# Seven products instead of eight for each 2x2 block in the second weights of the feed-forward and gated parts

## The chip, the cores and the metric

One Trainium2 chip, one NeuronCore of it. The metric is the device time of one execution of the whole program in microseconds (us); of several runs the median counts. One execution was also recorded by the hardware profiler, and all durations below come from that one.

## What is computed

Two small transformers, one after the other, on one sequence of 512 tokens with 1024 features, all in float32. The change touches four of their parts: twice `sqrelu_mlp` (4096 hidden features) and twice `swiglu` (2816 hidden features). Everything else (convolutions, three kinds of attention, norms) stays as it is.

```python
def sqrelu_mlp(h, w1, w2):
    return jnp.square(jax.nn.relu(h @ w1)) @ w2

def swiglu(h, w_gate, w_up, w_down):
    return (jax.nn.silu(h @ w_gate) * (h @ w_up)) @ w_down

# in both models, for each of two layers:
    h = rmsnorm(x, norm_ff_g[l]);  x = x + sqrelu_mlp(h, ff_w1[l], ff_w2[l])
    h = rms_norm(x, ffn_norm[i]);  x = x + swiglu(h, ffn_w_gate[i], ffn_w_up[i], ffn_w_down[i])
```

## The kernel before, in words

The activations lie transposed in SBUF: the residual `x` is eight tiles of 128 features by 512 tokens. A matmul takes 128x128 weights as its stationary operand and streams a 128x512 activation tile. Full float32 precision comes from splitting: each operand is a rounded high part (ScalarE, `nc.scalar.copy`) and the rest as a low part (VectorE, a subtraction), and `mm3` (line 171) issues three matmuls for each product: high x high, high x low, low x high. Each of the three loads its own weights.

`load_weights` (line 144) brings two columns of weight tiles (eight tiles deep, 1 MB) into one of three `raw` buffers. `split_weights` (line 161) makes `whi` on ScalarE (line 167) and `wlo` on VectorE (line 168). There are two tags, a and b, that alternate with every second call, with two buffers each; a new `whi` has to wait until TensorE has read the old contents of its buffer. `gemm_steps` (line 180) takes two output tiles at a time, goes over the hidden tiles k, and evacuates each PSUM bank at the end.

The feed-forward part (`ff_sqrelu`, line 672) goes over four chunks of eight hidden tiles. For each chunk it multiplies by the first weights (`ff_w1`), makes the hidden tiles (line 684 on VectorE, 686 on ScalarE, split at 215 and 216), and multiplies them by the second weights (`ff_w2`), adding the outcome to `x` (line 574 on VectorE). The gated part (`swiglu`, line 696) does the same with chunks of 8, 8 and 6 hidden tiles, where two first weights make each hidden tile. So the second weights of one chunk of eight are 8 x 8 products of 128x128 by 128x512, which are 192 matmuls.

A scheduler at build time puts the instructions of VectorE, ScalarE, GpSimd and the DMA queue into an order; TensorE's order is the program's. On the chip each engine takes its instructions in that order, and one that waits holds up those behind it.

Of the kernel before, what the change touches and what calls it, by code (L numbers as in the profile page):

```python
# [9 lines left out]
F32 = mybir.dt.float32  # L10
F32R = mybir.dt.float32r
# [69 lines left out]
def model_kernel(tc, a, c_mats, c_onehot, c_lnn, out):  # L81
# [497 lines left out]

    def memory_attention(l, st):  # L580
# [91 lines left out]
    def ff_sqrelu(l, st, last=None):  # L672
        nrm = Norm(st)
        with ExitStack() as s:
            ap = pool("fact", 22, s)
            fp = pool("fftmp", stack=s)
            h = [gained_act(hp_all, x[k], gain("norm_ff_g", l)[:, k : k + 1]) for k in range(KT)]
            st2 = Stats()
            for hc in range(FF1 // D):
                hid = []  # L680

                def evac(m, acc, hid=hid):
                    t = fp.tile([P, T], F32, name="t", tag="t", bufs=4)
                    nc.vector.scalar_tensor_tensor(t, acc, 0.0, nrm.b, op0=OP.max, op1=OP.mult)  # L684
                    u = fp.tile([P, T], F32, name="u", tag="u", bufs=4)
                    nc.scalar.activation(u, t, AF.Square)
                    hid.append(split_act(ap, u))

                gemm(cols(a["ff_w1"][l], 0, hc * D), h, evac, first=hc == 0, hooks=nrm.hooks() if hc == 0 else ())
                final = hc == FF1 // D - 1  # L690
                gemm(
                    cols(a["ff_w2"][l], hc * D, 0), hid, (last or residual(st2)) if final else residual(None), first=True
                )
        return st2

    def swiglu(l, st, last=None, finish=None):
        nrm = Norm(st)
        banks(4, 2, 2)
        with ExitStack() as s:
            ap = pool("gact", 22, s)  # L700
# [3 lines left out]
            wg, wu, wd = a["ffn_w_gate_2"][l], a["ffn_w_up_2"][l], a["ffn_w_down_2"][l]  # L704
            m0 = 0
            for n in (8, 8, 6):
                hid = []
                for j in range(n):
                    c = (m0 + j) * P
                    res = {}  # L710

                    def evac(m, acc, res=res, hid=hid):
                        if m == 0:
                            t = fp.tile([P, T], F32, name="t", tag="t", bufs=4)
                            nc.vector.tensor_tensor(t, acc, nrm.b, op=OP.mult)  # L715
                            g = fp.tile([P, T], F32, name="g", tag="g", bufs=4)
                            nc.scalar.activation(g, t, AF.Silu)  # L717
                            nc.gpsimd.tensor_tensor(g, g, nrm.b, op=OP.mult)  # L718
                            res[0] = g
                        else:  # L720
                            u = fp.tile([P, T], F32, name="u", tag="u", bufs=4)
                            nc.vector.tensor_tensor(u, acc, res[0], op=OP.mult)  # L722
                            hid.append(split_act(ap, u))
# [3 lines left out]
                final = m0 + n == FF2 // P  # L727
                n_cols = 6 if final and finish else KT
                gemm(cols(wd, m0 * P, 0, n_cols), hid, (last or residual(st2)) if final else residual(None), first=True)
                if n_cols < KT:  # L730
                    finish(cols(wd, m0 * P, n_cols * P, KT - n_cols), hid)
# [548 lines left out]
    with ExitStack() as s:  # L1280
        cp = pool("sconv", stack=s)
# [59 lines left out]
    def finish(specs, acts):  # L1341
# [23 lines left out]
        def tokens(half):  # L1365
            for t in range(2 * half, 2 * half + 2):
                for j in range(2):
                    b = bank("gs"[j])
# [51 lines left out]
```

## Time and profile before

| what | value |
|---|---|
| median of 3 runs | 2662.1 us (2660.45 to 2663.39) |
| the profiled execution's own time | 2659.51 us |
| its span, first to last instruction | 2657.7 us |
| TensorE busy | 2605.3 us, 98% of the span, 12521 matmuls |
| VectorE busy | 1489.1 us, 56% |
| ScalarE busy | 1096.9 us, 41% |
| GpSimd busy | 555.0 us, 21% |
| mean granted TensorE clock | 0.994 |

TensorE is busy nearly all the time, so time comes or goes only where its stream of matmuls gets shorter, gets slower, or has to wait. "Busy" of a matmul counts from its start to its modelled end, and neighbours overlap; the work that TensorE does is read from the distance between the starts of neighbours, not from the durations. A row of the timeline has start, duration, engine, line, operation, output and inputs, shape, count and, in brackets, the idle time before and what ended it.

### The profile page before, as it was taken

To read this page: it belongs to the slowest core of one execution; us is meant where nothing else is said; L and a number is where in the kernel's file an instruction comes from. 1 tells how busy PE (TensorE), PEld (TensorE's weight loads), DVE (VectorE), ACT (ScalarE), POOL (GpSimd) and SP (SyncE) were. 2 spreads that over 40 slices of the span, in tenths; PEclk is the share of its full clock that TensorE was granted. 3 is DMA by queue.
4 is the path that set the end of the run, shared out by engine and by line. 5 is a ranking of instruction groups with operands and counts; after the bars stand their busy time and mean duration, and the time that the engine had idled before them with its cause. 6 is when DMAs were issued, how large, how long until landed. Compare 5 with 4: busy or idle time off the path is not lost.

```text
span 2657.7 us, 32286 instructions
## 1 busy us (share of the span) xinstructions
PE 2605.3 (98%) x12521; PEld 2184.0 (82%) x12521; DVE 1489.1 (56%) x2215; ACT 1096.9 (41%) x1843; POOL 555.0 (21%) x586
## 2 busy tenths in 40 slices
PE   8999999999999999999999999999999999999999
PEld 6889888888878877888888788878888888788888
DVE  6995664443558887554344665343335777643333
ACT  6755443322337665442223323232224666422223
POOL 5862120000226532110000501111112221210111
PEclk9999999999999999999999999999999999999999
DMA  7255133233322322233333233843323323233331
GB/s 211 83 197 181 48 111 95 95 95 95 96 77 68 100 76 72 78 105 103 102 97 95 80 95 97 114 142 102 100 86 111 92 84 90 76 96 99 95 87 56
DMA packets 318057, 264.82 MB, mean 100 GB/s; under 512 B 6741, under 2 KB 304273, under 8 KB 317905
## 3 DMA queue, kind: packets, MB, share of 16 engines
q1 hardware_dynamic: 313808, 252.90, 31.3%
q0 software_dynamic: 1616, 5.52, 1.9%
q10 hardware_dynamic: 2480, 4.33, 0.5%
q8 instruction: 99, 1.62, 0.2%
q14 instruction: 54, 0.43, 0.0%
HBM read 251.16 MB, written 11.57 MB: 99 GB/s over the span
## 4 chain that ended last, share of the span: by engine, by line
PE 56%; DVE 2%; DMA 2%; issue 1%; ACT 1%; POOL 0%; ACTq 0%; DVEq 0%; POOLq 0%
PE ps_g L90 52%; DMA raw<-in_ffn_w_gate 2%; PE ps_s L90 2%; PE ps_t L90 1%; PE ps_t L93 1%; DVE wlo L168 0%; DVE x L1261 0%; DVE alo L228 0%; POOL ssq L252 0%; DVE x L574 0%; ACT ahi L227 0%; DVE x L1259 0%; DVE x L916 0%; ACT sq L248 0%; DVE wlo L773 0%
## 5 line engine op out<-in xcount | busy, mean ns | idle before, releaser
L90 PE MATMUL ps_g<-ahi,whi 128*128 128x512 f32 x3052 | 1196.5, 392 | 9.2 <-DVE x L574 4.9
L90 PE MATMUL ps_g<-ahi,wlo 128*128 128x512 f32 x3052 | 1190.2, 390 | 0.0
L90 PE MATMUL ps_g<-alo,whi 128*128 128x512 f32 x3052 | 1189.7, 390 | 0.0
L167 ACT CAST whi<-raw 128x1024 fp32r<-128x1024 f32 (+2 forms) x384 | 384.1, 1007 | 1115.2 <-PE ps_g L90 1035.3
L90 PEld LDWEIGHTS ps_g<-ahi,whi 128*128 128x128 f32 x3052 | 575.8, 189 | 127.8 <-issue 5.6
L90 PEld LDWEIGHTS ps_g<-ahi,wlo 128*128 128x128 f32 x3052 | 575.2, 188 | 121.7 <-DVE wlo L168 0.8
L90 PEld LDWEIGHTS ps_g<-alo,whi 128*128 128x128 f32 x3052 | 575.8, 189 | 115.4
L168 DVE TENSOR_TENSOR wlo<-raw,whi 128x1024 fp32r<-128x1024 f32 (+2 forms) x384 | 463.8, 1213 | 78.1 <-ACT whi L167 73.4
L574 DVE TENSOR_TENSOR x<-ps_g,x 128x512 f32<-128x512 f32 x144 | 99.2, 689 | 337.5 <-PE ps_g L90 337.4
L252 POOL TENSOR_TENSOR ssq<-ssq,sq 128x512 f32<-128x512 f32 x78 | 121.3, 1556 | 609.0 <-issue 313.7
L718 POOL TENSOR_TENSOR g<-g,rb 128x512 f32<-128x512 f32 x44 | 74.4, 1691 | 566.3 <-ACT g L717 566.3
L684 DVE SCALAR_TENSOR_TENSOR t<-ps_g,rb 128x512 f32<-128x512 f32 x64 | 44.1, 691 | 171.9 <-PE ps_g L90 171.9
L760 POOL TENSOR_TENSOR raw<-raw,gcols 128x512 f32<-128x512 f32 x48 | 53.9, 1147 | 304.3 <-DMA raw<-in_kvf_w 304.3
L414 POOL TENSOR_TENSOR pa<-pa,pr 128x512 f32<-128x512 f32 x80 | 111.8, 1400 | 18.7 <-ACT pa L410 8.2
L722 DVE TENSOR_TENSOR u<-ps_g,g 128x512 f32<-128x512 f32 x44 | 30.4, 691 | 141.9 <-PE ps_g L90 135.7
L406 DVE SCALAR_TENSOR_TENSOR ps_s<-u,gcols,ps_s 128x512 f32<-128x512 f32 x152 | 104.2, 744 | 0.2
L972 POOL TENSOR_SCALAR sall<-sall,rs 128x512 f32<-128x512 f32 (+3 forms) x128 | 75.9, 604 | 129.9 <-DVE rs L971 118.8
L773 DVE TENSOR_TENSOR wlo<-raw,whi 128x512 fp32r<-128x512 f32 x128 | 95.2, 772 | 13.5 <-ACT whi L770 13.4
L770 ACT CAST whi<-raw 128x512 fp32r<-128x512 f32 x128 | 74.1, 620 | 53.5 <-PE ps_g L90 47.4
L715 DVE TENSOR_TENSOR t<-ps_g,rb 128x512 f32<-128x512 f32 x44 | 30.4, 690 | 114.5 <-PE ps_g L90 114.5
L228 DVE SCALAR_TENSOR_TENSOR alo<-x,gcols,ahi 128x512 fp32r<-128x512 f32 x64 | 81.0, 1277 | 13.7 <-ACT ahi L227 13.7
L216 DVE TENSOR_TENSOR alo<-u,ahi 128x512 fp32r<-128x512 f32 x116 | 79.5, 689 | 1.4 <-ACT ahi L215 1.4
(245 smaller groups left out, 2843.7 us busy)
## 6 DMA issues: line engine op xcount, KB each, us to landing
raw<-in_ff_w SPq DMA_DIRECT2D x64, 1024.0 KB, 4.9
raw<-in_ffn_w_gate SPq DMA_DIRECT2D x44, 512.0 KB, 3.9
raw<-in_ffn_w_up SPq DMA_DIRECT2D x44, 512.0 KB, 5.2
raw<-in_ffn_w_down SPq DMA_DIRECT2D x16, 1024.0 KB, 5.1
raw<-in_conv_pw_w SPq DMA_DIRECT2D x16, 512.0 KB, 5.4
raw<-in_mem_wk SPq DMA_DIRECT2D x8, 1024.0 KB, 4.9
raw<-in_mem_wv SPq DMA_DIRECT2D x8, 1024.0 KB, 5.4
raw<-in_mem_wq SPq DMA_DIRECT2D x8, 1024.0 KB, 4.8
```

What stands on the lines that cost most here:

```text
L90: tc.keep_in_program_order(nc.tensor.matmul(*args, **kw))
L167: nc.scalar.copy(hi, view)
L168: nc.vector.tensor_tensor(lo, view, hi.bitcast(F32), op=OP.subtract)
L216: nc.vector.tensor_tensor(lo, src, hi.bitcast(F32), op=OP.subtract)
L228: nc.vector.scalar_tensor_tensor(lo, src, g, hi.bitcast(F32), op0=OP.mult, op1=OP.subtract)
L252: nc.gpsimd.tensor_tensor(self.ssq, self.ssq, dst, op=OP.add)
L406: nc.vector.scalar_tensor_tensor(acc, u[:, j : j + T], tapw(j), acc, op0=OP.mult, op1=OP.add)
L414: nc.gpsimd.tensor_tensor(pa, pa, pr, op=OP.add)
L574: nc.vector.tensor_tensor(x[m], acc, x[m], op=OP.add)
L718: nc.gpsimd.tensor_tensor(g, g, nrm.b, op=OP.mult)
L773: nc.vector.tensor_tensor(w[1][:, k0 : k0 + n, :], v, w[0][:, k0 : k0 + n, :].bitcast(F32), op=OP.subtract)
L972: pinned(nc.gpsimd.tensor_scalar(s, s, rs[:, i : i + 1], 1.0, op0=OP.mult, op1=OP.mult))
```

## The change

In every chunk but the last of each of the four parts (three of four in the feed-forward part, two of three in the gated part: ten chunks in all), the product with the second weights is made by a scheme of seven products (Strassen's, in Winograd's form) over blocks of two hidden tiles by two output tiles by two halves of the tokens (256 each). The weights of such a block are a11, a21, a12, a22 (row: even or odd hidden tile, column: first or second output tile).

- `Hidden` (line 596) holds one pair of hidden tiles: `quarters` (line 616) keeps three of the four quarters and makes four differences and sums of them on VectorE, then splits all seven into `hi` and `lo`. In the last chunk `tile` (line 611) splits the whole tile as before.
- `Seven` (line 631) holds four accumulators in SBUF. `weights` (line 638) makes, for a pair of output tiles and four pairs of hidden tiles, four groups in the order b (a11), a (a12, a22), then after a subtraction on GpSimd (line 644) and three sums on VectorE (645 to 647) c and d. That is 3584 elements per partition to split where there were 2048.
- `add` (line 652) goes over the four pairs of output tiles, j = 0 to 3. Each has 7 products x 4 hidden pairs x 3 matmuls = 84 matmuls of 128x256, into the two halves of four banks A, B, C, D. For j = 0 the order is changed so that the fourth hidden pair comes last for all seven products.
  A row of `SEVEN` names the weight group, the column in it, the quarter or sum of the hidden pair, the bank and the half of the bank.
- `evac` (line 674) adds B to `x`, subtracts half of D from it, and copies (first chunk, ScalarE, line 685) or adds (later chunks, VectorE, line 683) A and C to the accumulators. `combine` (line 687) adds the accumulators to `x` after the last such chunk, six steps on VectorE for each j.
- PSUM is cut into six general banks and two others in these parts (`banks(6, 0, 2)`), instead of three or four general ones.

```diff
+    SEVEN = (
+        ("b", None, 0, "A", 1),
+        ("a", 0, 2, "B", 1),
+        ("a", 1, 6, "D", 1),
+        ("c", 1, 4, "C", 1),
+        ("c", 0, 3, "C", 0),
+        ("d", 1, 5, "A", 0),
+        ("d", 0, 1, "B", 0),
+    )
...
+        def quarters(self):
+            f = self.raw
+            d = self.ap.tile([P, 4, HALF], F32, name="bdif", tag="bdif", bufs=1)
+            nc.scalar.copy(self.hi[:, 0:3, :], f[:, 1:4, :])
+            nc.vector.tensor_tensor(
+                d[:, 0:2, :], f[:, 1:3, :], f[:, 0:1, :].to_broadcast([P, 2, HALF]), op=OP.subtract
+            )
+            nc.vector.tensor_tensor(d[:, 2, :], f[:, 2, :], d[:, 0, :], op=OP.add)
+            nc.vector.tensor_tensor(d[:, 3, :], d[:, 2, :], f[:, 3, :], op=OP.subtract)
+            nc.scalar.copy(self.hi[:, 3:7, :], d)
+            for part, src in ((slice(0, 3), f[:, 1:4, :]), (slice(3, 7), d)):
+                nc.vector.tensor_tensor(
+                    self.lo[:, part, :], src, self.hi[:, part, :].bitcast(F32), op=OP.subtract
+                )
...
+        def weights(self, src, r0, j, h):
+            raw = load_weights([(src, r0, 2 * j * P), (src, r0, (2 * j + 1) * P)], 2 * h)
+            v = raw[:, 0 : 2 * h, :].rearrange("p (i a) n -> p i a n", a=2)
+            even, odd = v[:, :, 0, :], v[:, :, 1, :]
+            a11, a21, a12, a22 = even[:, :, 0:P], even[:, :, P:], odd[:, :, 0:P], odd[:, :, P:]
+            w = {"b": split_weights(a11, [P, h, P]), "a": split_weights(odd, [P, h, 2 * P])}
+            nc.gpsimd.tensor_tensor(a21, a11, a21, op=OP.subtract)
+            nc.vector.tensor_tensor(a22, a22, a21, op=OP.subtract)
+            nc.vector.tensor_tensor(a11, a22, a11, op=OP.add)
+            nc.vector.tensor_tensor(a12, a12, a22, op=OP.subtract)
+            w["c"] = split_weights(even, [P, h, 2 * P])
+            w["d"] = split_weights(odd, [P, h, 2 * P])
+            return w
...
+                order = [(i, k) for i in range(7) for k in range(h)]
+                if j == 0:
+                    order.sort(key=lambda ik: ik[1] == h - 1)
+                for i, k in order:
+                    grp, at, b, name, half = SEVEN[i]
+                    opens = name not in ps
+                    if opens:
+                        ps[name] = bank("g")
+                    wk = [z[:, k, :] if at is None else z[:, k, at * P : (at + 1) * P] for z in w[grp]]
...
+                    closes = k == h - 1 and (name, half) in (("A", 0), ("B", 0), ("C", 0), ("D", 1))
+                    mm3(ps[name][:, half * HALF : (half + 1) * HALF], wk, act, opens, closes)
+                    if closes:
+                        self.evac(j, name, ps[name])
...
     def ff_sqrelu(l, st, last=None):
...
-                final = hc == FF1 // D - 1
-                gemm(
-                    cols(a["ff_w2"][l], hc * D, 0), hid, (last or residual(st2)) if final else residual(None), first=True
-                )
+                if final:
+                    gemm(cols(a["ff_w2"][l], hc * D, 0), parts, last or residual(st2), first=True)
+                else:
+                    seven.add(a["ff_w2"][l], hc * D, hid)
+                    if hc == FF1 // D - 2:
+                        seven.combine()
```

`swiglu` is changed in the same way, with `combine` after its second chunk.

The order of instructions moves in three places that matter below. In the names, the number behind `raw` tells the pair of output tiles, and `whi` and `wlo` are the high and low parts of a weight group.

First, ScalarE in the second weights of a chunk. Before, at the end of the first chunk's hidden tiles and in its second weights:

```order
L167 CAST whi_3957<-raw_3955 128x1024
L167 CAST whi_3961<-raw_3955 128x1024
L167 CAST whi_4019<-raw_4017 128x1024
L167 CAST whi_4023<-raw_4017 128x1024
L167 CAST whi_4081<-raw_4079 128x1024
L167 CAST whi_4085<-raw_4079 128x1024
```

Now, in the second chunk of the first feed-forward part, from the end of the hidden tiles on; `raw_4705` is j = 1 and `raw_4819` is j = 2, and the rows are b and a of j = 1, b and a of j = 2, c and d of j = 1, c of j = 2:

```order
L625 CAST bhi_4552<-bdif_4583 128x1024
L167 CAST whi_4707<-raw_4705 128x512
L167 CAST whi_4711<-raw_4705 128x1024
L167 CAST whi_4821<-raw_4819 128x512
L167 CAST whi_4825<-raw_4819 128x1024
L167 CAST whi_4719<-raw_4705 128x1024
L167 CAST whi_4723<-raw_4705 128x1024
L167 CAST whi_4833<-raw_4819 128x1024
```

Before, the weights of one pair of tiles followed those of the pair ahead. Now two groups of j = 2 stand in front of the last two groups of j = 1. The same order stands in the second chunk of the other feed-forward part, and in the chunk with `combine` of all four parts.

Second, ScalarE in the first chunk of the first feed-forward part (`raw_3949` is j = 1, `raw_4063` is j = 2), where the accumulators are filled by copies:

```order
L167 CAST whi_3951<-raw_3949 128x512
L167 CAST whi_3955<-raw_3949 128x1024
L685 COPY acc0_3515<-ps_g_3887 128x512
L685 COPY acc0_3515<-ps_g_3857 128x512
L167 CAST whi_4065<-raw_4063 128x512
L167 CAST whi_3963<-raw_3949 128x1024
L167 CAST whi_4069<-raw_4063 128x1024
L167 CAST whi_3967<-raw_3949 128x1024
```

Here only b of j = 2 stands in front of c of j = 1. The first chunks of all four parts have this order.

Third, VectorE. Before, in the second weights, evacuations and low parts alternate:

```order
L574 TENSOR_TENSOR x2_80<-ps_g_3903,x2_80 128x512
L168 TENSOR_TENSOR wlo_4020<-raw_4017,whi_4019 128x1024
L574 TENSOR_TENSOR x3_81<-ps_g_3904,x3_81 128x512
L168 TENSOR_TENSOR wlo_4024<-raw_4017,whi_4023 128x1024
L574 TENSOR_TENSOR x4_82<-ps_g_3965,x4_82 128x512
```

Now, in the third chunk of the first feed-forward part, the one with `combine`, from b of j = 2 (`raw_5575`) to c of j = 1 (`raw_5461`):

```order
L168 TENSOR_TENSOR wlo_5578<-raw_5575,whi_5577 128x512
L645 TENSOR_TENSOR raw_5461<-raw_5461 128x4x128
L691 TENSOR_TENSOR acc0_3515<-acc0_3515 128x256
L692 TENSOR_TENSOR x0_78<-x0_78,acc0_3515 128x512
L646 TENSOR_TENSOR raw_5461<-raw_5461 128x4x128
L647 TENSOR_TENSOR raw_5461<-raw_5461 128x4x128
L695 TENSOR_TENSOR x1_79<-x1_79,acc0_3515 128x512
L677 TENSOR_TENSOR x3_81<-x3_81,ps_g_5509 128x256
L693 TENSOR_TENSOR x0_78<-x0_78,acc0_3515 128x256
L168 TENSOR_TENSOR wlo_5582<-raw_5575,whi_5581 128x1024
L168 TENSOR_TENSOR wlo_5476<-raw_5461,whi_5475 128x1024
```

Steps of `combine` for j = 0, an evacuation and two low parts of j = 2 now stand in front of the low part of c of j = 1. In the second chunk of the feed-forward parts the order is the same without the four rows of lines 691 to 695.

## Rows read from the trace of the kernel before

**Rows 1.** What TensorE waited for, 360 to 700 us: total us, times, longest.

```profile
PE ps_g L90 <- DVE x L574: 0.5, 1, 0.5
```

**Rows 2.** Timeline of TensorE, second weights of the first chunk: start, duration.

```profile
423.75 0.39 PE L90 MATMUL ps_g<-ahi,wlo 128*128 128x512 f32 x1
...
439.84 0.39 PE L90 MATMUL ps_g<-alo,whi 128*128 128x512 f32 x1
```

**Rows 3.** Timeline of TensorE, last two output tiles, 256 tokens at a time.

```profile
2637.80 0.28 PE L90 MATMUL ps_g<-ahi,whi 128*128 128x256 f32 x1
...
2641.28 0.28 PE L90 MATMUL ps_g<-ahi,wlo 128*128 128x256 f32 x1
```

**Rows 4.** Groups by shape, weight loads in front of 128x256 matmuls: busy us, mean ns.

```profile
L90 PEld LDWEIGHTS ps_g<-wlo,ahi 128*128 128x128 f32 x256 | 49.0, 191 | 0.5 <-DVE wlo L773 0.2
```

**Rows 5.** Groups by shape, VectorE and ScalarE, 370 to 700 us: busy us, mean ns.

```profile
L168 DVE TENSOR_TENSOR wlo<-raw,whi 128x1024 fp32r<-128x1024 f32 x60 | 73.0, 1223 | 8.1 <-ACT whi L167 8.1
...
L574 DVE TENSOR_TENSOR x<-ps_g,x 128x512 f32<-128x512 f32 x32 | 22.0, 689 | 83.9 <-PE ps_g L90 83.9
...
L168 DVE TENSOR_TENSOR wlo<-raw,whi 128x512 fp32r<-128x512 f32 x4 | 2.7, 681 | 0.0
...
L167 ACT CAST whi<-raw 128x1024 fp32r<-128x1024 f32 x60 | 62.8, 1054 | 200.4 <-PE ps_g L90 200.4
...
L167 ACT CAST whi<-raw 128x512 fp32r<-128x512 f32 x4 | 2.5, 619 | 4.8 <-PE ps_g L90 4.7
```

**Rows 6.** Timeline of VectorE: two pairs in a row, and a 256-wide step.

```profile
400.43 1.31 DVE L684 SCALAR_TENSOR_TENSOR t<-ps_g,rb 128x512 f32<-128x512 f32 x2 [4.34 <-PE ps_g L90]
401.66 2.35 DVE L168 TENSOR_TENSOR wlo<-raw,whi 128x1024 fp32r<-128x1024 f32 x2
...
2640.16 0.42 DVE L1354 TENSOR_TENSOR x<-ps_g,x 128x256 f32<-128x256 f32 x1 [1.46 <-PE ps_g L90]
```

**Rows 7.** Timeline, all engines, around the end of one hidden tile.

```profile
411.28 0.39 PE L90 MATMUL ps_g<-alo,whi 128*128 128x512 f32 x1
411.51 0.39 PE L90 MATMUL ps_g<-ahi,wlo 128*128 128x512 f32 x1
411.71 1.05 ACT L167 CAST whi<-raw 128x1024 fp32r<-128x1024 f32 x1 [3.20 <-PE ps_g L90]
...
411.93 0.69 DVE L684 SCALAR_TENSOR_TENSOR t<-ps_g,rb 128x512 f32<-128x512 f32 x1 [2.70 <-PE ps_g L90]
...
412.79 1.22 DVE L168 TENSOR_TENSOR wlo<-raw,whi 128x1024 fp32r<-128x1024 f32 x1 [0.17 <-ACT whi L167]
```

**Rows 8.** Stretches of 1 us: length, PE, PEld, DVE, ACT, POOL busy, clock, DMA.

```profile
885.00:886.00 1.00, 0.24 (x1) 0.24 (x2) 0.71 (x2) 0.00 (x0) 0.77 (x2) 0.65 0.00 0
886.00:887.00 1.00, 1.00 (x6) 1.00 (x6) 0.00 (x0) 0.30 (x1) 1.00 (x2) 0.50 0.00 0
887.00:888.00 1.00, 1.00 (x6) 1.00 (x5) 0.68 (x2) 1.00 (x3) 0.71 (x1) 0.50 0.00 0
888.00:889.00 1.00, 1.00 (x4) 0.76 (x4) 0.61 (x2) 1.00 (x3) 0.00 (x0) 0.64 0.00 0
```

**Rows 9.** Timeline of TensorE: the waits ahead of the two clock stretches.

```profile
184.07 1.13 PE L90 MATMUL ps_t<-u,ones 128*128 128x512 f32 x2 [2.69 <-DVE u L416]
...
885.76 2.18 PE L93 MATMUL ps_t<-mats,sall 128*128 128x128 f32 x9 [2.42 <-POOL sall L972]
```

**Rows 10.** Stretch of 1 us after the first of these waits, columns as in rows 8.

```profile
185.00:186.00 1.00, 1.00 (x10) 0.96 (x9) 0.76 (x2) 0.04 (x1) 0.00 (x0) 1.00 1.08 386
```

**Rows 11.** The page's costliest groups: a slower low part, and a GpSimd step.

```profile
L718 POOL TENSOR_TENSOR g<-g,rb 128x512 f32<-128x512 f32 x44 | 74.4, 1691 | 566.3 <-ACT g L717 566.3
...
L773 DVE TENSOR_TENSOR wlo<-raw,whi 128x512 fp32r<-128x512 f32 x128 | 95.2, 772 | 13.5 <-ACT whi L770 13.4
```

More of the change, by code (lines that the diff above doesn't have):

```diff
@@ L578, in residual, with flat, __init__, place @@
         return evac
+    SEVEN = (
[7 more added lines that the diff above has]
+    )
+    HALF = T // 2
+    def flat(v):
+        return v.rearrange("p a b -> p (a b)")
+    class Hidden:
+        def __init__(self, ap):
+            self.ap = ap
+            self.hi = ap.tile([P, 7, HALF], F32R, name="bhi", tag="bhi", bufs=4)
+            self.lo = ap.tile([P, 7, HALF], F32R, name="blo", tag="blo", bufs=4)
+            self.raw = ap.tile([P, 4, HALF], F32, name="braw", tag="braw", bufs=3)
+        def place(self, e):
+            return flat(self.raw[:, 2 * e : 2 * e + 2, :])
+        def tile(self, e):
+            hi, lo = (flat(z[:, 2 * e : 2 * e + 2, :]) for z in (self.hi, self.lo))
+            split_into(hi, lo, self.place(e))
+            return hi, lo
+        def quarters(self):
[12 more added lines that the diff above has]
+                )
@@ L704, in swiglu, with evac @@
             wg, wu, wd = a["ffn_w_gate_2"][l], a["ffn_w_up_2"][l], a["ffn_w_down_2"][l]
+            seven = Seven(fp)
             m0 = 0
             for n in (8, 8, 6):
-                hid = []
+                hid, parts = [], []
+                final = m0 + n == FF2 // P
                 for j in range(n):
                     c = (m0 + j) * P
-                    res = {}
-                    def evac(m, acc, res=res, hid=hid):
+                    if j % 2 == 0:
+                        hid.append(Hidden(ap))
+                    def evac(m, acc, hd=hid[-1], parts=parts, final=final, e=j % 2):
+                        g = hd.place(e)
@@ L725, in swiglu @@
                     first = m0 + j == 0
                     gemm([(wg, 0, c), (wu, 0, c)], h, evac, first=first, hooks=nrm.hooks() if first else ())
[L727 to L731, printed above, removed]
+                if final:
+                    n_cols = 6 if finish else KT
+                    gemm(cols(wd, m0 * P, 0, n_cols), parts, last or residual(st2), first=True)
+                    if finish:
+                        finish(cols(wd, m0 * P, n_cols * P, KT - n_cols), parts)
+                else:
+                    seven.add(wd, m0 * P, hid)
+                    if m0:
+                        seven.combine()
@@ L1280, in model_kernel @@
     with ExitStack() as s:
+        banks(4, 2, 2)
         cp = pool("sconv", stack=s)
```

75 lines of the change are left out of this document (57 added, 18 removed).

## The prediction

> **What bounds the kernel now.** I looked first at the page's busy shares: TensorE is at work for 98% of the span. Then at its waits in the first feed-forward part: 0.5 us in 340 us [rows 1]. So these parts are one unbroken stream of matmuls, and the price of a matmul is the distance between two starts. In the timeline, 71 such distances take 439.84 - 423.75 = 16.09 us, or 0.2267 us for 128x512 [rows 2]. Half as wide, 29 distances take 2641.28 - 2637.80 = 3.48 us, or 0.1200 us [rows 3]: more than half, since some 13 ns of each don't shrink with the width. Every one of these has a weight load of its own, listed at 191 ns [rows 4], so the loads lie beside the stream. The other engines have room: VectorE 56%, ScalarE 41%.
>
> **What the change removes.** Take one pair of output tiles and one pair of hidden tiles. Before: 4 products of 3 matmuls at 512, 12 x 0.2267 = 2.72 us. Now: 7 of 3 at 256, 21 x 0.1200 = 2.52 us. That is 0.20 us less (7.4%, not Strassen's 12.5%). A chunk has 4 x 4 of these, ten chunks have 160: **32.0 us saved**, if TensorE never waits.
>
> The Trainium skill (TensorE: Matmul & The Clock Gate, Back-to-back issue gap) gives the distance of isolated warm matmuls as N/2.4 + 2.5 ns. By it the saving would be 12 x 215.8 - 21 x 109.2 = 297 ns a block, 47 us in all, as an estimate; rows 2 and 3 are longer by 11 ns each, and they decide.
>
> **What the change adds, and its cover.** Durations: a VectorE step on 1024 elements 1.22 us, on 512 0.68, on 256 0.42 [rows 5, 6]; for 768 I take 0.95, between them. Back to back the next starts some 0.07 us before the row ends (two of 1.22 take 2.35) [rows 6]. ScalarE: 1.05 for 1024, 0.62 for 512 [rows 5], 0.84 for 768. From one engine's end to the other's start it is 0.03 to 0.04 us, and a high part starts that long after the last matmul that reads its old buffer: 411.28 + 0.39, then 411.71 [rows 7]. 128x256 matmuls end 0.28 after their start [rows 3].
>
> For each j, VectorE has four low parts (0.68 + 3 x 1.22), three sums (2.04) and the evacuations (0.42 + 3 x 0.69): 8.9 us of TensorE's 84 x 0.12 = 10.08. That fits, but leaves no room where `combine` adds 4 x 0.42 + 2 x 0.68 = 3.0. The seven quarters of the last hidden pair cost nothing: counted from the start of the chunk's first seven-product matmul, evacuation 0.19 to 0.88, low part of d to 2.2, then 0.68, 0.95, 0.42, 0.42, ScalarE's 1.05 and 1.22 end at about 6.9; with the fourth pair sorted last they are wanted at 63 x 0.12 + 0.12 = 7.68. If that cover went, each chunk would wait for the rest. GpSimd's subtraction (1.7 us at most [rows 11]) runs a j ahead. DMA moves what it moved. The new cut of PSUM I count at nothing: the first banks of a part are wanted only after its norm.
>
> **The waits I expect: j = 1.** Because of the sorted order, the buffers of j = 0 all come free late. A high part waits for its buffer, and j = 2 uses those of j = 1. Times from the chunk's first seven-product matmul; j = 0 ends at 10.08.
>
> Second chunk of the feed-forward parts (2 chunks). Buffer a is free at 8.68; high part 8.71 to 9.76. Its low part stands on VectorE behind two accumulator sums, the second of which needs bank A (9.88): 10.86 to 12.08. TensorE wants it at 11.76 and waits **0.35**. Then the order on ScalarE bites: a of j = 2 stands ahead of c of j = 1, and its buffer is free only when a of j = 1 has been used up, near 14.8. So a runs 14.82 to 15.87 and c 15.90 to 16.95. TensorE, done with a at 14.75, waits **2.23** for c, does two matmuls, and waits for the low part of c, which VectorE makes after that of a: 17.04 to 18.26, **1.07**. Sum 3.65 us.
>
> The chunk with `combine` (4 chunks). As far as a, the same. But VectorE has five steps of `combine`, three weight sums and an evacuation between the low part of a (j = 1) and that of a (j = 2): with their starts a little overlapped they end at 17.8, the low part of a at 19.0, that of c at 20.14. TensorE waits 0.35 + 2.24 + **2.94** = 5.53 us.
>
> First chunks (4 chunks). No accumulator sums on VectorE, and only b of j = 2 ahead of c: c high 13.57 to 14.62 where 14.40 is wanted (0.25); low behind an evacuation, 14.95 to 16.17, **1.31**. Sum 1.56 us.
>
> For j = 2 and 3 the buffers come free in turn; the same walk leaves 1 to 4 us to spare there, also with `combine`, whose last steps end under the next first weights.
>
> Waits: 2 x 3.65 + 4 x 5.53 + 4 x 1.56 = **35.7 us**. No row of before has these queues, so the bounds: at least what the ScalarE order alone forces in six chunks, 2.2 + 1.07, together 20 us; at most 15% more than walked, 41 us, if the steps run like the 0.77 us low parts instead of 0.68 [rows 11].
>
> **The clock.** After TensorE had waited 2.42 us for GpSimd [rows 9], the granted clock fell to its lower level (0.5, 1.2 GHz) and stayed there for a while; over the four stretches the missing share is 0.35 + 0.5 + 0.5 + 0.36 = 1.7 us of work [rows 8]. After a wait of 2.69 us elsewhere it did not fall [rows 9, 10]. So a wait of this size costs 0 or 1.7 us more. The six chunks with waits over 2 us have two close together; I take one fall each, **10.2 us** (bounds 0 and 20).
>
> **The sum.** -32.0 + 35.7 + 10.2 = +13.9 us on the profiled execution's 2659.5: 2673.4. The median is 2.6 above that execution, so I forecast **2676 us**, 0.5% slower. This case's own range goes from just above the first rival below to both upper bounds (2662.1 - 32 + 41 + 20): 2667 to 2692.
>
> **Rivals.**
> 1. The same waits, but the clock holds: 2662.1 - 32.0 + 35.7 = 2666, no difference that can be told. For it: rows 10. Against: two waits in a row per chunk.
> 2. Faster: the waits shrink to what ScalarE's order forces. Its place is the low part of c on VectorE in j = 1: if it is done by 4.56 us after j = 1 starts (three products and two matmuls), or directly after c's high part, nothing else is lost. Then 2662 - 32 + 20 = 2650, and 2630 if even that is covered. For it: VectorE is idle for 1.5 us around 7 to 8.6 and a little overlap more per step adds up. Against: the order of the ScalarE queue is fixed, and the buffer really is in use.
> 3. VectorE becomes the bound where `combine` runs: with steps at 0.77 instead of 0.68 a j takes 12.2 us of VectorE against 10.08, for three j in four chunks 25 us: 2700.
> 4. The Trainium skill (the same page, Part 3, The mechanism) says that a weight load overlaps a running matmul only where it goes to other rows of the array. These loads take all rows; nine more of them in the open, 191 ns each, are 1.72 us a block, 275 us in all: about 2940. Rows 3 and 4 speak against it, as 191 ns don't fit into 120 otherwise.
>
> **Numbers.** Forecast 0.60, rival 1 0.14, rival 2 0.14, rival 3 0.11, rival 4 0.01. A measurement of this kernel tells 0.2%, 5 us, from no change. Slower holds the forecast and rivals 3 and 4: 0.72; within 0.2% rival 1: 0.14; faster rival 2: 0.14. The range takes in the forecast, rival 1, the slower end of rival 2 and the nearer half of rival 3: 2648 to 2698.
>
> **What would show it.** Matmuls in the new stretches 0.120 us apart; 1440 matmuls more; TensorE waiting in j = 1 of every such chunk, first for a `whi` (line 167), then for a `wlo` (line 168), in all near 36 us, most where `combine` runs; a chunk's 336 matmuls taking 40.3 us plus 1.6, 3.7 or 5.5; the granted clock at 0.5 behind the longer waits. The prediction is wrong if those waits are below 25 us, if they stand elsewhere (the quarters of the last pair, PSUM banks at the start of a part), or if half-wide matmuls with their loads are further apart than 0.12 us.

## The result and the profile after

The changed kernel takes **2701.9 us** (median of 4 runs, 2698.2 to 2705.3) against 2661.6 in the runs beside it: a ratio of 1.0151, with a 95% interval of 1.0138 to 1.0165. The forecast was 2676 with a range of 2648 to 2698: the direction was right, the size was not, and the time lies above the range. The profiled execution is the slowest of the four, so the 45.8 us that its span grew, which are taken apart below, are more than the 40.3 us between the medians.

| what | before | after |
|---|---|---|
| the profiled execution's own time, us | 2659.5 | 2705.3 |
| its span | 2657.7 | 2703.5 |
| TensorE busy | 2605.3, 98% | 2601.1, 96%, 13961 matmuls |
| VectorE busy | 1489.1 | 1782.3, 66% |
| ScalarE, GpSimd busy | 1096.9, 555.0 | 1203.9, 608.7 |
| mean granted clock | 0.994 | 0.983 |

VectorE has 293 us more to do and is still idle a third of the time. TensorE has 1440 matmuls more and no more busy time. So the 46 us between the two spans are idle time and a slower clock. The waits of TensorE in the changed kernel (total us, times, longest):

```profile
PE ps_g L90 <- ACT whi L167: 26.1, 11, 12.6
PE ps_g L90 <- DVE wlo L168: 20.3, 17, 2.5
...
PE ps_t L90 <- POOL rtm L270: 6.8, 3, 2.3
...
PE ps_g L90 <- DVE x L574: 5.2, 3, 2.3
PE ps_t L90 <- POOL ssq L252: 5.1, 2, 4.1
PE ps_g L90 <- DVE x L1393: 4.1, 1, 4.1
```

The page's costliest groups (busy us, mean ns, idle before and its releaser) tell which of the first two lines belong to the seven products; their operands are `bhi` and `blo`:

```profile
L90 PE MATMUL ps_g<-ahi,whi 128*128 128x512 f32 x2176 | 860.3, 395 | 23.0 <-ACT whi L167 12.6
...
L90 PE MATMUL ps_g<-bhi,wlo 128*128 128x256 f32 (+1 forms) x1356 | 415.2, 306 | 18.9 <-DVE wlo L168 18.9
L90 PE MATMUL ps_g<-bhi,whi 128*128 128x256 f32 (+1 forms) x1356 | 413.9, 305 | 13.5 <-ACT whi L167 13.5
```

Inside the seven products TensorE idles 32.4 us, for the casts and the low parts of the weights, as forecast. But a single wait of 12.6 us belongs to an ordinary matmul (`ahi`), and the waits for `rtm`, `x` and `ssq` stand where a part begins. To see how much lies where, I took the distances between the first matmuls of the stages in both traces:

| stage | before, us | after, us |
|---|---|---|
| second weights, first chunk of a part (4 of them) | 43.52 | 41.98, 41.98, 42.21, 42.24 |
| second chunk of a feed-forward part (2) | 43.52 | 47.30, 46.93 |
| chunk with `combine` (4) | 43.52 | 48.58, 48.60, 49.43, 47.91 |
| sum of these ten | 435.2 | 457.2 |
| first `w1` chunk of the two feed-forward parts | 46.1, 46.1 | 49.5, 49.4 |
| first gate and up products, first and second gated part | 96.8, 90.3 | 106.9, 93.9 |
| short convolution | 185.5 | 187.0 |

The ten chunks take 22.0 us more (the forecast's net was 13.9). The entries of the parts take another 3.4 + 3.3 + 10.0 + 3.6 + 1.5 = 21.8 us, where the forecast had nothing. Of the last 2.0 us up to 45.8, 1.9 are at the start (383.6 us, before 381.8), which the change doesn't touch: after the wait that [rows 9] show there (2.69 us before, 2.7 now) the granted clock was at 0.5 for 3.4 us this time. The start took 381.3 to 383.7 us in the profiles of all kernels here.

**Inside a chunk.** The timeline of TensorE (start, duration) in the chunk that begins at 615.0 us, in its second block:

```profile
629.87 0.28 PE L90 MATMUL ps_g<-bhi,wlo 128*128 128x256 f32 x1
632.11 0.39 PE L90 MATMUL ps_g<-bhi,whi 128*128 128x256 f32 x1 [1.97 <-ACT whi L167]
632.34 0.28 PE L90 MATMUL ps_g<-blo,whi 128*128 128x256 f32 x1
635.08 0.58 PE L90 MATMUL ps_g<-bhi,wlo 128*128 128x256 f32 x1 [2.46 <-DVE wlo L168]
635.46 0.41 PE L90 MATMUL ps_g<-bhi,whi 128*128 128x256 f32 x1
```

First a cast, two matmuls, then a low part: this is the place that the prediction walked to. ScalarE and VectorE at that time:

```profile
630.07 2.94 ACT L167 CAST whi<-raw 128x1024 fp32r<-128x1024 f32 x3 [2.88 <-PE ps_g L90]
```

```profile
632.68 2.34 DVE L168 TENSOR_TENSOR wlo<-raw,whi 128x1024 fp32r<-128x1024 f32 x2
```

ScalarE waits 2.88 us for the buffer of a (j = 2), then casts a and only then c and d of j = 1. VectorE makes the low part of a (j = 2) ahead of that of c, and ends at 635.02. The idle times in brackets count from the modelled end of the matmul before, 0.28 us after its start. The prediction counts from when the next one could have started, 0.12 after it, so each wait is 0.16 us longer by its count: 2.12 and 2.62 us here, for its 2.24 and 2.94.

Behind these waits the durations are 0.41 instead of 0.28. The stretches of 1 us (columns as in [rows 8]) show why:

```profile
633.00:634.00 1.00, 0.00 (x0) 0.00 (x0) 1.00 (x2) 0.01 (x1) 0.00 (x0) 1.00 0.00 0
634.00:635.00 1.00, 0.00 (x0) 0.00 (x0) 1.00 (x2) 0.00 (x0) 0.00 (x0) 0.73 0.00 0
635.00:636.00 1.00, 0.92 (x4) 0.92 (x5) 1.00 (x3) 0.00 (x0) 0.00 (x0) 0.50 0.00 0
...
640.00:641.00 1.00, 1.00 (x6) 1.00 (x6) 0.69 (x1) 0.91 (x1) 0.00 (x0) 0.50 1.01 352
641.00:642.00 1.00, 1.00 (x9) 1.00 (x9) 0.83 (x1) 0.14 (x1) 0.00 (x0) 0.86 0.13 43
```

The granted clock falls to 0.5 while TensorE waits and stays there for 6.8 us; in [rows 8] it was 3.4 us. It happens once in each of the six chunks with the longer waits (five times for 6.8 us, once for 3.4) and in none of the four others. Summed over all distances between neighbouring matmuls of the ten chunks, 3360 x 0.120 = 403.2 us are the stream itself, 36.5 us are gaps by the prediction's count (32.4 us idle) and 17.4 us are matmuls further apart without a gap, 16.7 of them in those six chunks: 2.8 us for each fall.

**At the entries.** GpSimd at the start of the first feed-forward part, and what TensorE does then:

```profile
399.66 1.26 POOL L644 TENSOR_TENSOR raw<-raw 128x512 f32<-128x512 f32 x1 [4.23 <-DMA raw<-in_ff_w]
400.88 1.02 POOL L270 TENSOR_TENSOR rtm<-ms,mhalf 128x4 f32<-128x4 f32 x1
```

```profile
401.95 1.74 PE L90 MATMUL ps_t<-mats,rtm 128*128 128x128 f32 x8 [2.23 <-POOL rtm L270]
```

The subtraction of second weights (line 644) waits for its DMA, and the norm's power step (line 270) stands behind it in the queue. In the first gated part, ScalarE:

```profile
1753.31 0.83 ACT L619 CAST bhi<-braw 128x768 fp32r<-128x768 f32 x1 [31.63 <-DMA gd<-gt]
1754.05 1.04 ACT L167 CAST whi<-raw 128x1024 fp32r<-128x1024 f32 x1
```

```profile
1755.14 0.80 PE L90 MATMUL ps_g<-ahi,whi 128*128 128x512 f32 x1 [12.61 <-ACT whi L167]
```

A cast into a hidden tile waits 31.6 us for a DMA that has nothing to do with it: the broadcast of the bias rows (5.2 MB, 53.9 us from issue to landing), whose source tile had lain in the memory that the new hidden tile got. The weights' casts queue behind.

At the short convolution and at the second gated part, TensorE waits at the fourth matmul of the part, the first into its second bank, for a step on VectorE that reads an output of the part before:

```profile
1513.51 0.77 PE L90 MATMUL ps_g<-ahi,whi 128*128 128x512 f32 x1 [4.14 <-DVE x L1393]
...
2325.81 0.80 PE L90 MATMUL ps_g<-ahi,whi 128*128 128x512 f32 x1 [2.27 <-DVE x L574]
```

### The profile page after: what moved, and what is told of

Same layout as the page of the kernel before. It is cut to its first block, busy times and chain, and to the rows that moved or that the text cites. A ratio compares the mean times of both kernels' runs of the same rounds, so it can differ in the third digit from the quotient of the medians.

```text
span 2703.5 us, 35674 instructions
## 1 busy us (share of the span) xinstructions
PE 2601.1 (96%) x13961; PEld 2247.0 (83%) x13961; DVE 1782.3 (66%) x2679; ACT 1203.9 (45%) x1955; POOL 608.7 (23%) x626
## 4 chain that ended last, share of the span: by engine, by line
PE 54%; DVE 4%; another core or an unknown queue 1%; issue 1%; ACT 1%; DMA 0%; POOL 0%; ACTq 0%; DVEq 0%; POOLq 0%
PE ps_g L90 50%; PE ps_s L90 2%; DVE wlo L168 1%; PE ps_t L90 1%; PE ps_t L93 1%; DVE alo L228 0%; DVE x L1395 0%; DVE x L574 0%; ACT ahi L227 0%; ACT whi L167 0%; DMA raw<-in_ff_w 0%; DVE x L1393 0%; DVE x L1050 0%; DVE wlo L907 0%
## 5 line engine op out<-in xcount | busy, mean ns | idle before, releaser
L90 PE MATMUL ps_g<-ahi,whi 128*128 128x512 f32 x2176 | 860.3, 395 | 23.0 <-ACT whi L167 12.6
L90 PE MATMUL ps_g<-ahi,wlo 128*128 128x512 f32 x2176 | 853.1, 392 | 1.5 <-DVE wlo L168 1.4
L90 PE MATMUL ps_g<-alo,whi 128*128 128x512 f32 x2176 | 853.3, 392 | 0.0
L90 PEld LDWEIGHTS ps_g<-alo,whi 128*128 128x128 f32 x2176 | 412.2, 189 | 82.1
L90 PE MATMUL ps_g<-bhi,wlo 128*128 128x256 f32 (+1 forms) x1356 | 415.2, 306 | 18.9 <-DVE wlo L168 18.9
L90 PE MATMUL ps_g<-bhi,whi 128*128 128x256 f32 (+1 forms) x1356 | 413.9, 305 | 13.5 <-ACT whi L167 13.5
L90 PE MATMUL ps_g<-blo,whi 128*128 128x256 f32 (+1 forms) x1356 | 412.6, 304 | 0.0
L90 PEld LDWEIGHTS ps_g<-bhi,wlo 128*128 128x128 f32 x1356 | 266.5, 197 | 30.7 <-DVE wlo L168 22.4
L90 PEld LDWEIGHTS ps_g<-bhi,whi 128*128 128x128 f32 x1356 | 266.5, 197 | 24.2 <-ACT whi L167 15.5
L90 PEld LDWEIGHTS ps_g<-blo,whi 128*128 128x128 f32 x1356 | 266.2, 196 | 8.6
```

What stands on the lines that cost most here:

```text
L90: tc.keep_in_program_order(nc.tensor.matmul(*args, **kw))
```

## The experiments

The theory: each piece of the loss hangs on a place, in a queue or in memory, not on an engine's load. Its rivals are VectorE's load, dearer half-wide matmuls, and costs that only move on. Ratios are to the kernel before, timed beside each; its median moved by 2 us between the groups of runs, so across groups the ratios compare better than the times. Chunk lengths are from the profiles (a mean for each kind).

| kernel | us | ratio, 95% | first / second / combine chunks | sum of ten |
|---|---|---|---|---|
| before | 2659.6 to 2661.6 | 1 | 43.5 / 43.5 / 43.5 | 435.2 |
| changed | 2701.9 | 1.0151 (1.0138 to 1.0165) | 42.1 / 47.1 / 48.6 | 457.2 |
| e_order | 2685.5 | 1.0088 (1.0073 to 1.0103) | 42.0 / 42.4 / 46.3 | 438.0 |
| e_act | 2684.8 | 1.0091 (1.0078 to 1.0105) | 42.0 / 42.6 / 45.7 | 436.2 |
| e_defer | 2673.5 | 1.0047 (1.0033 to 1.0061) | 42.1 / 42.5 / 43.0 | 425.1 |
| e_nosort | 2700.4 | 1.0150 (1.0132 to 1.0169) | 44.4 / 44.0 / 46.4 | 451.0 |
| e_rtm | 2699.7 | 1.0140 (1.0125 to 1.0155) | 43.2 / 45.7 / 49.1 | 460.3 |
| e_pow | 2692.8 | 1.0120 (1.0106 to 1.0134) | 42.1 / 45.0 / 47.7 | 449.5 |
| e_gd | 2693.0 | 1.0115 (1.0098 to 1.0131) | 43.0 / 46.8 / 48.0 | 457.7 |
| e_cut | 2700.2 | 1.0143 (1.0128 to 1.0158) | 42.2 / 46.4 / 48.2 | 454.0 |
| e_all | 2651.3 | 0.9965 (0.9953 to 0.9978) | 42.6 / 42.5 / 43.0 | 427.3 |
| e_early | 2648.8 | 0.9959 (0.9945 to 0.9972) | 42.1 / 42.3 / 42.8 | 424.1 |

**e_order: the order of the casts and low parts.** `behind` adds an edge that fixes the order of issue on one engine and waits for nothing; `self.turns` starts as `[None, None]`, and all four splits of a block get it.

```diff
+    def behind(turns, *two):
+        for i, ins in enumerate(two):
+            if turns[i] is not None:
+                tc.add_manual_dep(ins.ins, turns[i].ins.name, mybir.DependencyInfo(mybir.DependencyClass.NoSync, mybir.DependencyReason.DATA), reason="behind")
+            turns[i] = ins
...
-        nc.scalar.copy(hi, view)
-        nc.vector.tensor_tensor(lo, view, hi.bitcast(F32), op=OP.subtract)
+        one = nc.scalar.copy(hi, view)
+        two = nc.vector.tensor_tensor(lo, view, hi.bitcast(F32), op=OP.subtract)
+        if turns is not None: behind(turns, one, two)
...
-            w["c"] = split_weights(even, [P, h, 2 * P])
+            w["c"] = split_weights(even, [P, h, 2 * P], self.turns)
```

> Edit: in the seven-product blocks the cast and the low part of a block's first group may not be issued ahead of those of the last group of the block before (issue order only; the instructions are the same). Theory (the wait in the second block comes from the order of ScalarE's and VectorE's queues: the casts for the third block stand ahead of those for c and d of the second): the six chunks of the middle and combine kinds fall from 46.9-49.4 us to about 42, the 32.4 us of waits of half-wide matmuls on whi and wlo fall below 6, no clock fall is left in the ten chunks, and the time falls by about 37 us, to 2665. Rival 1 (VectorE's load is the bound, 3 more passes per hidden pair and the combine): the same load in another order leaves the combine chunks above 46 and the time above 2690. Rival 2 (the half-wide matmuls themselves cost more than 0.120 us): the waits go but the chunks stay above 44. The entries outside the chunks (49.5 and 48.6 us for the first chunks of the ff parts, 106.9 and 93.9 for the gated ones) stay as they are under all three.

The middle chunks fell to 42.4, as the theory has it, and rival 2 is out: 42.4 is 40.3 plus gaps and a little. The combine chunks fell only to 45.0 to 48.3 (rival 1 said above 46, but also a time above 2690), in three of the four the clock still falls, and the time fell by 16 us instead of 37. The second block of the first of them, which begins at 607.7 us:

```profile
624.31 0.39 PE L90 MATMUL ps_g<-bhi,whi 128*128 128x256 f32 x1 [1.33 <-ACT whi L167]
626.16 0.58 PE L90 MATMUL ps_g<-bhi,wlo 128*128 128x256 f32 x1 [1.35 <-DVE wlo L168]
```

So a second cause is at work where `combine` runs.

**e_act: ScalarE's order alone.** As e_order, but

```diff
-        if turns is not None: behind(turns, one, two)
+        if turns is not None: behind(turns, one)
```

> Edit: as e_order, but only ScalarE's casts are held to the order; VectorE's queue is left to the scheduler. Theory (the casts for the third block ahead of those of the second are the cause, VectorE's low parts follow the casts): nearly all of e_order's gain stays, the middle chunks at 42 to 43 us, the time 2684 to 2689. Rival (VectorE's own order holds the low parts back): the middle chunks stay at 44 or more and the time above 2692.

All of e_order's gain stays. But the two edits led to one program: in the two traces every engine takes the same steps in the same order, VectorE included. So it is enough to hold the casts, and the scheduler moves the low parts along with them; how much VectorE's order does by itself is not shown. That ScalarE's order made the cast of c late is read from the row at 630.07 above. As one program measured twice, the two also show that the sum of the ten chunks varies by 1.8 us from profile to profile.

**e_defer: where `combine` stands.** e_order, and

```diff
-                nc.vector.tensor_tensor(acc[:, 0, :], acc[:, 0, :], acc[:, 1, :], op=OP.add)
+                behind([self.turns[1]], nc.vector.tensor_tensor(acc[:, 0, :], acc[:, 0, :], acc[:, 1, :], op=OP.add))
```

> Edit: the order of e_order, and besides the first pass of each combine may not be issued on VectorE ahead of the low part of the chunk's last group, so that the 24 passes stand in the chunk's last block and the next first weights. e_order left 45.7, 48.3, 45.0 and 46.1 us in the combine chunks beside 42.4 in the middle ones. Theory (what is left there is combine's passes standing among the low parts on VectorE in the first blocks, a matter of place): the four chunks fall to about 42.4, no clock fall is left in them, the next first weights stay at 43.6 (87.1, 65.3), and the time falls by about 15 us from e_order's 2685.5, to 2670. Rival (VectorE's load bounds: the passes only push what follows): the gain in the chunks comes back as waits in the chunk behind them and the time stays above 2680.

The four chunks fell to 43.0, the first weights behind them stayed at 43.55, 87.07 and 65.31 us, and the time is 2673. The same passes, issued a block or two later, cost nothing: not VectorE's load, but their place ahead of low parts that TensorE wants. The longest single wait in the ten chunks is now 1.4 us, and no clock fall is left in them.

**e_nosort: the cover of the quarters.** The last hidden pair's products are no longer sorted to the end of the first block.

```diff
-                if j == 0:
-                    order.sort(key=lambda ik: ik[1] == h - 1)
```

> Edit: the changed kernel without the sort that puts the products of the last hidden pair at the end of a chunk's first block. Theory (the sort is the cover of the last pair's quarters, whose last pass ends some 6.9 us after the start of the chunk; without it the first product's fourth pair is wanted at 1.1 us): TensorE waits near 5 to 6 us in every chunk's first block, the casts of the second block come earlier (their buffers are free sooner, so 1 to 2 us of its waits go), the clock falls in all ten chunks, and the time rises by 40 to 70 us from 2701.9. Rival (the quarters come in time anyway, the sort only holds the weight buffers longer): the chunks become shorter by the 1.5 us of the second block's wait, and the time falls by 10 us or more.

Both expectations failed. TensorE does wait in the first block, but for less than I had said, as the first products need only the first of the two casts and low parts; in the chunk that begins at 1366.7 us:

```profile
1369.22 0.38 PE L90 MATMUL ps_g<-bhi,whi 128*128 128x256 f32 x1 [1.24 <-ACT bhi L619]
1370.55 0.38 PE L90 MATMUL ps_g<-blo,whi 128*128 128x256 f32 x1 [0.95 <-DVE blo L627]
```

The second block's waits go in return, since its buffers come free earlier. First chunks get 2.3 us longer on average, as the clock now falls in three of the four, at 1.4 us each; the others get 2 to 3 us shorter; and the time is the changed kernel's within the intervals. The clock falls in seven of the ten chunks, not in all. So the sort covers a wait in the first block and makes one in the second.

**e_rtm and e_pow: GpSimd's queue.** e_rtm keeps both steps behind all that stands before them in the program; e_pow holds the subtraction behind the last power step (kept in `power[0]`) and nothing else. First e_rtm's edit, then e_pow's:

```diff
-            nc.gpsimd.tensor_tensor(a21, a11, a21, op=OP.subtract)
+            pinned(nc.gpsimd.tensor_tensor(a21, a11, a21, op=OP.subtract))
...
-        nc.gpsimd.tensor_tensor(r, ms, mhalf[:, 0:n], op=OP.pow)
+        pinned(nc.gpsimd.tensor_tensor(r, ms, mhalf[:, 0:n], op=OP.pow))
```

```diff
-        nc.gpsimd.tensor_tensor(r, ms, mhalf[:, 0:n], op=OP.pow)
+        power[0] = nc.gpsimd.tensor_tensor(r, ms, mhalf[:, 0:n], op=OP.pow)
...
-            nc.gpsimd.tensor_tensor(a21, a11, a21, op=OP.subtract)
+            behind([power[0]], nc.gpsimd.tensor_tensor(a21, a11, a21, op=OP.subtract))
```

> Edit: on GpSimd the power step of the norm and the first subtraction of second weights keep the order of the program, so the norm's step stands first. Theory (the entry of both ff parts waits because that subtraction, which waits for its weights' DMA, stands ahead of the norm's step on GpSimd): the two waits of 2.2 and 2.3 us on rtm go, the first chunks of the two ff parts fall from 49.5 and 48.6 us to about 46.1, and the time falls by about 6 us, to 2696. Rival (the entries wait for banks, because the PSUM is cut anew there): the waits stay under another name and the time stays within 1.5 us of 2702.

> Edit: on GpSimd the subtraction of second weights may not be issued ahead of the power step of the part's norm, and nothing else is held; e_rtm held the subtraction behind everything before it, and its gated parts lost 2.2 us in each first chunk of second weights, where the subtraction then stood behind the last gate product. Theory: the first chunks of the ff parts are 45.4 us as in e_rtm, the chunks of second weights of the gated parts stay at 42.2, and the time is 7 to 8 us below 2701.9, 2694 to 2695. Rival (those 2.2 us were of something else): 2699 to 2700 as e_rtm.

Both bring the entries to 45.35 us, from 49.5 and 49.4. In e_pow nothing else moves on any queue, and GpSimd's rows at that place are now

```profile
396.57 1.02 POOL L270 TENSOR_TENSOR rtm<-ms,mhalf 128x4 f32<-128x4 f32 x1 [1.75 <-DVE ms L268]
399.05 1.28 POOL L644 TENSOR_TENSOR raw<-raw 128x512 f32<-128x512 f32 x1 [1.46 <-DMA raw<-in_ff_w]
```

e_rtm's time fell by only 2 us, where 6 were expected. In e_rtm the first chunks of the gated parts went from 42.2 to 44.4 us: there the subtraction, held behind all before it, came behind the last gate product. In e_pow they are 42.2 and 42.4. The edge has to name what it must not overtake, not more. (e_pow's total fell 1 us further than its entries, as some of its combine and second chunks were shorter this time; see the last section.)

**e_gd: memory.** The accumulators, which are written late, go where the bias rows lay:

```diff
-            ap = pool("gact", stack=s)
             fp = pool("gtmp", stack=s)
+            ap = pool("gact", stack=s)
```

> Edit: the two pools of the gated part are opened in the other order, so that the accumulators (first written after the first chunk) and not the halved hidden tiles lie where the source of the bias broadcast lay. Theory (ScalarE's first cast of a fourth hidden pair waits 31.6 us for the 5.2 MB broadcast to leave that memory, and the weight casts queue behind it): the 12.6 us wait of TensorE goes, the first gate and up products of the first gated part fall from 106.9 us to about 96, and the time falls by about 10 us, to 2692. Rival (ScalarE is simply loaded there: three passes per hidden pair more): the wait of TensorE stays above 8 us and the time above 2699.

The 12.6 us wait is gone, the stage takes 95.6 us instead of 106.9 (96.8 before the change), and the time fell as expected. Some 3 us of it came back in the next stage: that chunk of second weights went from 42.2 to 45.5, with new waits of 1.26 us for a low part of weights and 0.87 us for one of the last hidden pair, which are no longer made during the long wait. In the stage of the gate and up products itself, a weight tile still comes late while the broadcast runs, as before the change: TensorE waits 2.5 us for its cast (4.3 before).

**e_cut: the cut of PSUM.**

```diff
-        banks(6, 0, 2)
+        if l: banks(4, 2, 2)
...
-                        ps[name] = bank("g")
+                        ps[name] = bank("s" if name in "CD" and psum["bufs"]["s"] else "g")
...
-        banks(4, 2, 2)
         cp = pool("sconv", stack=s)
```

> Edit: the short convolution and the first gated part go on with the cut of PSUM that the ff part left (no new cut), and the second gated part has four banks of the first kind and two of the second as before the change, the seven products taking C and D from the second. Theory (at a new cut the second bank of the first two lies on the bank of the last output of the part before, so TensorE waits for that output's addition, 4.1 us at the short convolution and 2.3 us at the second gated part, and the clock falls behind the second): the short convolution is 1.5 us shorter, the first gate and up products of the second gated part fall from 93.9 to about 90.3, and the time falls by about 5 us, to 2697. Rival (those waits are of the additions themselves, which are late whatever bank): no change, 2701 to 2703.

At the second gated part the theory holds: the wait of 2.27 us for the last output is gone and the stage is 2.0 us shorter (91.85). The other 1.6 us of its 3.6 stay: the clock is at 0.5 there for 3.4 us, which it wasn't before the change. At the short convolution the outcome is the rival's: the stage stays at 186.8, and TensorE now waits for the sums of squares instead, which come from the same late outputs:

```profile
1515.51 1.05 PE L90 MATMUL ps_t<-ones,ssq 128*128 128x1 f32 x8 [1.58 <-POOL ssq L252]
1517.86 1.76 PE L90 MATMUL ps_t<-ones,ssq 128*128 128x1 f32 x8 [1.29 <-POOL ssq L252]
```

How much the new cut costs there stays open, as that stage takes 186.1 to 187.5 us in the profiles that keep the cut and 185.2 to 186.8 in those without it. The whole time moved too little (1.7 us) to be told from the changed kernel.

**e_all and e_early: together.** e_all is e_defer, e_pow, e_gd and e_cut; e_early besides holds the subtraction that empties bank D behind the same block's low part of c (kept in `self.low`):

```diff
-                nc.vector.tensor_tensor(xo[:, HALF:], xo[:, HALF:], b[:, HALF:], op=OP.subtract)
+                behind(self.low, nc.vector.tensor_tensor(xo[:, HALF:], xo[:, HALF:], b[:, HALF:], op=OP.subtract))
```

> Edit: e_defer, e_pow, e_gd and e_cut together. Theory (each cost is separate and hangs on a place in a queue or in memory): the ten chunks take about 423 us (457 in the changed kernel, 435 before), the entries what they took in e_pow, e_gd and e_cut, and the sum comes to 2646 to 2652, below the 2661.5 of the kernel before. Rival (the costs move to the next late thing when one goes): above 2656.

> Edit: e_all, and besides the subtraction that empties bank D may not stand on VectorE ahead of the same block's low part of c. In e_all each chunk still waits 1.4 us for that low part in its second block: the cast of c ends 0.85 us before the low part starts, and VectorE waits in between for bank D. Theory: those waits fall by 0.4 to 0.9 us in each of the ten chunks, to near 41.2 us in the first chunks, and the time falls by 4 to 9 us from e_all's 2651.3, to 2642 to 2647. Rival (the low part then only moves to the next late thing, the high part's own chain of three sums): within 2 us of 2651.

e_all is faster than both kernels: 0.9965 of the kernel before, with the time that was expected. Its ten chunks take 427.3 us and not 423, as the first chunk of the first gated part is 44.2 us, much as in e_gd. TensorE's waits in it:

```profile
PE ps_g L90 <- DVE wlo L168: 13.1, 17, 1.4
...
PE ps_g L90 <- ACT whi L167: 4.3, 7, 3.2
...
PE ps_t L90 <- POOL rtm L270: 2.2, 1, 2.2
```

e_early shortens the first chunks of the feed-forward parts by 0.8 us as expected, to 41.2, and the other chunks by 0.1 to 0.4. In the two traces the ten chunks differ by 3.2 us and the medians by 2.5: less than expected, and with intervals that overlap. Its median is the lowest here, 0.4% below the kernel before; whether it beats e_all is not shown.

## Why the prediction was right and wrong

- **The price of a matmul, and the saving of 32.0 us: right.** In a stretch without waits of the changed kernel's first chunk, 74 distances take 448.68 - 439.80 = 8.88 us, 0.1200 each:

```profile
439.80 0.28 PE L90 MATMUL ps_g<-blo,whi 128*128 128x256 f32 x1
...
448.68 0.28 PE L90 MATMUL ps_g<-bhi,whi 128*128 128x256 f32 x1
```

  Rival 4 (weight loads in the open) is out. The Trainium skill (TensorE: Matmul & The Clock Gate, Back-to-back issue gap) has a formula for isolated warm matmuls that comes to 109 ns at this width, as an estimate. The trace doesn't agree, with 120 ns, and the measurement decides.
- **The waits of 35.7 us: right in place and in sum.** The gaps between matmuls of the ten chunks sum to 36.5 us: 1.47 to 1.73 in first chunks (1.56 forecast), 3.73 and 4.02 in second ones (3.65), 5.27 to 5.86 with `combine` (5.53). That they agree so closely is in part luck, as errors of the walk cancel. Where `combine` runs, the wait for the low part of c was 2.6 us and not 2.94. The first wait of the six longer chunks was 0.5 to 1.1 us and not 0.35: the low part of b ahead of it took 0.89 to 1.71 us and not 0.68, as GpSimd's subtraction ran beside it (last section). e_order and e_defer take away the two causes that the walk named: the cast of a (j = 2) ahead of that of c (j = 1) on ScalarE, and combine's passes ahead of low parts on VectorE.
- **The clock, 10.2 us: mechanism right, size wrong.** One fall in each of the six chunks, as taken, but 2.8 us each, 16.7 in all; so rival 1 (the clock holds) is out. The price came from one fall that lasted 3.4 us [rows 8]; five of these lasted 6.8. Inside its bounds of 0 and 20, but 6.5 us of the miss.
- **The step that failed** is the paragraph of what costs nothing: GpSimd's subtraction "runs a j ahead", "DMA moves what it moved", and "The new cut of PSUM I count at nothing: the first banks of a part are wanted only after its norm". The subtraction ran so far ahead that it stood before the norm's step in GpSimd's queue (6.7 us at two entries). The DMA moved the same bytes, but a new tile lay where its source had been (10.0 us). And the second bank is wanted at a part's fourth matmul, long before the norm (3.6 us at one entry, 2.0 of which e_cut took back; at the short convolution 1.5, whose cause stays open). That is 21.8 us that no bound of the range held. In the profiled execution the miss is 45.8 - 13.9 = 31.9 us: these 21.8, the clock's 6.5, the waits' 0.8, and 1.9 at the start, where the clock fell in this execution. PSUM banks at the start of a part stand in the prediction's own list of signs against it. The walk had followed ScalarE's and VectorE's queues, but not GpSimd's. One sign was in the trace before: TensorE waited 4.3 us in the first gated part, while the same broadcast ran, then for weights that came late.
- **The quarters of the last pair at nothing:** no wait on them in the changed kernel, but e_nosort shows that the reason given was not the whole of it: the sort that covers them makes the second block's wait.
- **Rival 2** (less waiting for the low part of c) did not come by itself: the low part waited as walked. A sum of chunks near its 423 us (435.2 - 32 + 20) came in e_defer, 425.1 us, and its time is that of e_all, where the entries are mended too; both got there by another way, with the queues put in another order. **Rival 3** (VectorE as the bound) is out by e_defer. Its 2700 us is the nearest to the measured 2701.9, by coincidence.
- **Two slips in the prediction's figures**, which change nothing here: 2662.1 - 32 + 41 + 20 is 2691 and not 2692, and rival 3's 12.2 us for a j don't follow from the terms given, where 8.9 + 3.0 us at 0.68 become 13.5 at 0.77.

## What to carry over

Count a chunk by the distance of its matmuls and then walk the queues that feed it, but walk the first stage of each part too: a step added to any queue can be hoisted ahead of a step that everything waits for. When a change adds tiles or cuts memory anew, ask whose memory they get and what may still be reading it. When the scheduler's order is the cause, it helps to name just the one step that must not be overtaken: here such an edge gave all of the loss back, and a broader one only part of it.

## What was not expected of the hardware

- **The same waits, with and without a fall of the clock.** In e_pow the second chunk, at 519.4 us, has waits of the changed kernel's length at the same place, 1.97 and 0.95 us, and the clock stays at 1.00 behind them; the chunk takes 44.2 us instead of 47.3. In e_gd the same chunk has these two waits too, its gaps are the same in sum (3.5 us, in e_pow 3.6), and the clock falls for 6.8 us; it takes 46.8. Two to three us behind the waits, first e_pow, then e_gd:

```profile
540.00:541.00 1.00, 1.00 (x11) 1.00 (x10) 0.94 (x3) 0.22 (x1) 0.00 (x0) 1.00 0.39 81
```

```profile
544.00:545.00 1.00, 1.00 (x6) 1.00 (x6) 0.10 (x1) 0.00 (x0) 0.00 (x0) 0.50 0.74 165
```

  Shorter pairs had both outcomes as well: 1.33 and 1.35 us in e_order's combine chunks (a fall in three of four), 1.24 and 0.95 us in e_nosort (a fall in the first chunk, at 438.3 us, none in the second, at 526.4). What decides is open.
- **VectorE and GpSimd hold each other up: the step that starts later waits.** A low part of 512 elements, 0.68 us in [rows 5], took 1.80 in e_gd where a GpSimd step began just before it; the next, of 1024, took 1.85 instead of 1.22:

```profile
1787.56 1.80 DVE L168 TENSOR_TENSOR wlo<-raw,whi 128x512 fp32r<-128x512 f32 x1
...
1789.88 1.85 DVE L168 TENSOR_TENSOR wlo<-raw,whi 128x1024 fp32r<-128x1024 f32 x1
```

```profile
1787.51 1.30 POOL L847 TENSOR_TENSOR braw<-braw,rb 128x512 f32<-128x512 f32 x1 [6.34 <-ACT braw L846]
1789.36 1.29 POOL L644 TENSOR_TENSOR raw<-raw 128x512 f32<-128x512 f32 x1 [0.55 <-DVE wlo L168]
```

  In this trace, the 51 low parts of 512 elements beside no GpSimd step of 512 take 0.67 to 0.69 us. The 13 that start while such a step runs take 0.69 to 1.80: what is left of that step, and 0.55 to 0.56 us. The 8 in whose course such a step starts are not longer; there GpSimd's own step is: its subtraction takes up to 1.67 us, and 1.26 to 1.30 alone. The Trainium skill (GPSIMD Engine Reference, Specifications) says that the two share their interfaces to SBUF, with contention where a VectorE instruction has two inputs there; these rows agree.
- The attention between the two feed-forward parts took 396.0 us before, 396.5 to 398.6 in the other profiles, and 401.7 in e_gd, which doesn't touch it. The clock accounts for most of that: it was granted at 0.5 for 30.7 us of the stage in e_gd and for 20.5 us before, which is 5.1 of the 5.7 us.
